# A decoder layer's matrix-state recurrence: its small products issued by array shape

## The chip, the cores and the metric

The kernel runs on one core of a Trainium2 chip. A core has a matrix engine (PE, or TensorE: a 128 x 128 array that multiplies a loaded operand with a streamed one and writes to the accumulation memory, PSUM), a vector engine (DVE), a scalar engine (ACT), a general engine (POOL) and a queue engine (SP); each runs its own instructions in order, and they wait for one another by semaphores. PSUM has eight banks of 128 partitions x 512 fp32. The metric is the device time of one execution, in microseconds.

## What is computed

One layer of a hybrid decoder, for a prompt of 1,024 tokens and for 8 sampled sequences of 8 new tokens each. The input projection feeds three groups of heads; their outputs are projected back, then come a squared-ReLU MLP and a gated embedding. The group that matters here is the first, an RWKV-7 recurrence with a 64 x 64 state per head and four heads:

```python
def wkv7_scan(r, decay, k, v, a_vec, b_vec, s0):
    def step(s, inp):
        r_t, w_t, k_t, v_t, a_t, b_t = inp
        sa = jnp.einsum('bhvk,bhk->bhv', s, a_t)
        s = (s * w_t[:, :, None, :] + sa[..., None] * b_t[:, :, None, :]
             + v_t[..., None] * k_t[:, :, None, :])
        y = jnp.einsum('bhvk,bhk->bhv', s, r_t)
        return s, y
    xs = tuple(jnp.moveaxis(t, 1, 0) for t in (r, decay, k, v, a_vec, b_vec))
    s_final, ys = lax.scan(step, s0, xs)
    return jnp.moveaxis(ys, 0, 1), s_final
```

The prompt starts from a zero state, the sampled sequences from a state that is given. The other two groups are a short gated convolution and stick-breaking attention over the prompt, and over 512 cached tokens for the samples. All of it is fp32; large products are split into a high and a low part in a reduced format and run as three products.

## The kernel before

The kernel is one long program. Its pieces are written down in an order that gives priorities; a planner then fixes the order of each engine's instructions ahead of the run, from its own estimate of every instruction's length: an instruction is placed when its operands and its buffers are free by that estimate, and the earlier one in the text goes first. So independent work fills the gaps: while the recurrence waits for a copy, PE runs matmuls of the projections.

In time, the input norm and the recurrence's inputs come first (to about 195 us), then the prompt's recurrence together with the projections for attention (line 898, and from 376 us the convolution's, lines 171 to 173), then the sampled state (434 to 545 us) together with the convolution and the first attention blocks, then attention, the cached tokens, the MLP (from line 1140) and the last gate.

The recurrence runs over the prompt in 16 chunks of 64 tokens, two at a time (a pair, chunks e = 0 and 1). Heads are kept in pairs: head h = 2j + s, with s the upper or lower 64 partitions.

- `wkv_local` (line 490) prepares a pair without the state. Its first products (line 535) multiply the two kinds of keys (`bk`, 64 rows, 2 x 64 columns) with two streamed rows (`ar`, 64 x 128) for every e, j and s: eight matmuls, those of s = 0 into one bank and those of s = 1 into another, each filling 128 partitions; DVE masks each bank into `AB` (line 538). Transposes (544, 552) and small products (559 to 589) lead to `UV` and `Wm`, and line 600 forms `Rm` and `FT`, one bank for each e. All of this takes turns on PSUM banks 3 and 4, which two such generators share; `TT`, `ar`, `bk`, `AB`, `UV`, `Rm` and `FT` have three buffers.
- `wkv_chain` (line 640) carries the state from chunk to chunk. Line 648 forms the additions to the state (banks 6 and 7). The output of both chunks is collected in one tile of bank 5: for each e and j, line 656 puts in the local part (`UV` with `AB`, all 128 rows of the array, 64 columns, a pair of heads in the two column halves) and line 659 adds the state's part (`St` with `Rm`, 64 rows and 64 columns, a pair of heads on the diagonal quarters). Line 665 multiplies the state by `FT`, and DVE finishes the new state (line 668). Line 673 copies the output, and `wkv_out` normalises it.
- `wkv_sample_chunk` (line 714) does one chunk of 64 sampled tokens. It has PSUM bank 2 alone for everything. It transposes the given states (line 734, loaded into `s_in`), runs `wkv_local` with one chunk, forms the outputs (743, 747), and then, for each j, spreads `UV` and `AB` over the eight sequences with a mask (`um`, line 756; `bmk`, line 762), multiplies them (759: 128 rows; 763: 64 rows, both heads in the upper rows and in the two column halves, with 512 elements streamed each), and finishes the new states (765 to 783). `s_in`, `um`, `FTs` and `so` share two buffers (tag um); `bmk` has one of its own, so that the second `bmk` is made when the first has been read.

A matmul in fp32 leaves two records each for weight load and product in the trace. The transposes of lines 544 and 552 use the whole array.

Of the kernel before, what the change touches and what calls it, by code (L numbers as in the profile page):

```python
# [21 lines left out]
F32 = mybir.dt.float32  # L22
# [10 lines left out]
NB = 8  # L33
# [15 lines left out]
def hybrid_step(ctx: ExitStack, tc: tile.TileContext, I, O):  # L49
    nc = tc.nc  # L50
    V, S, G, PE, SP = nc.vector, nc.scalar, nc.gpsimd, nc.tensor, nc.sync
# [181 lines left out]
    for s in range(2):  # L233
        hs = slice(64 * s, 64 * s + 64)
# [165 lines left out]
    for j in range(2):  # L400
# [9 lines left out]
        for i in range(9):  # L410
            e = min(T, 128 * i + 128)
# [67 lines left out]
    def hp(h):  # L479
        return slice(64 * (h % 2), 64 * (h % 2) + 64)  # L480
# [9 lines left out]
    def wkv_local(cs, res, local, sample=False):  # L490
# [11 lines left out]
        ar = kp.tile([128, ne, 2, 3, 64], F32, name="ar", bufs=1 if sample else 3)  # L502
        bk = kp.tile([128, ne, 2, 2, 64], F32, name="bk", bufs=1 if sample else 3)
# [21 lines left out]
        AB = kp.tile([128, ne, 4, 192], F32, name="AB", bufs=1 if sample else 3)  # L525
        mk = mfull[:, 1 if sample else 0].rearrange("p a t -> p (a t)")[:, None, None, :].to_broadcast([128, ne, 2, 128])

        for both in ((0,), (1,)) if sample else ((0, 1),):
            p4s = {s: local().rearrange("p (e j c) -> p e j c", e=2, j=2) for s in both}
            for e in E:  # L530
                for j in range(2):
                    for s in both:
                        hs = slice(64 * s, 64 * s + 64)
                        ra = ar[hs, e, j, 0:2] if e == 0 else ar[hs, e, j, 2:0:-1]
                        PE.matmul(p4s[s][:, e, j, :], bk[hs, e, j].rearrange("p a t -> p (a t)"), ra,  # L535
                                  start=True, stop=True)
            for s in both:
                V.tensor_mul(AB[:, 0:ne, s:4:2, 64:192], p4s[s][:, 0:ne], mk)
        yield
# [7 lines left out]
        UV = kp.tile([128, ne, 4, 64], F32, name="UV", bufs=1 if sample else 3)  # L547
# [36 lines left out]
        p4 = h4(psv, 512)  # L584
# [13 lines left out]
        for h in range(4):  # L598
            for e in E:
                PE.matmul(j2(prfs[e], 256)[hp(h), h // 2, :], Wm[es(e), h, :], AB[es(e), e, h, 0:128],  # L600
                          start=True, stop=True)
# [37 lines left out]

    def wkv_chain(c, AB, UV, Wm, Rm, FT):  # L640

        py = ybank()
        p4 = py[:, :256].rearrange("p (e j t) -> p e j t", e=2, j=2)
        pg = chain()
        g4 = pg[:, :256].rearrange("p (e j t) -> p e j t", e=2, j=2)
        for e in range(2):
            for h in range(4):
                PE.matmul(g4[hp(h), e, h // 2, :], AB[:, e, h, 0:64], UV[:, e, h, :], start=True, stop=True)
        PG = kp.tile([128, 2, 2, 64], F32, name="PG", bufs=2)
        V.tensor_mul(PG, g4, pcs[:, :, c:c + 2].rearrange("p j e -> p e j")[:, :, :, None].to_broadcast([128, 2, 2, 64]))  # L650
        yield
        for e in range(2):
            St = state[0]
            for j in range(2):
                for h in (2 * j, 2 * j + 1):
                    PE.matmul(p4[hp(h), e, j, :], UV[:, e, h, :], AB[:, e, h, 64:128], start=True, stop=St is None)
                if St is not None:
                    for h in (2 * j, 2 * j + 1):
                        PE.matmul(p4[hp(h), e, j, :], St[hp(h), j, :], Rm[hp(h), e, j, :], start=False, stop=True)
            if St is None:  # L660
                state[0] = PG[:, e]
                continue
            pf = chain()
            for h in range(4):
                PE.matmul(j2(pf)[hp(h), h // 2, :], FT[hp(h), e, h // 2, :], St[hp(h), h // 2, :], start=True, stop=True)
            Sn = kp.tile([128, 2, 64], F32, name="St", bufs=3)
            for j in range(2):
                V.scalar_tensor_tensor(Sn[:, j, :], j2(pf)[:, j, :], pcs[:, j, c + e:c + e + 1], PG[:, e, j, :],
                                       op0=ALU.mult, op1=ALU.add)
            state[0] = Sn  # L670
            yield
        Yg = kp.tile([128, 2, 128], F32, name="Yg", bufs=2)
        S.copy(Yg.rearrange("p j (e t) -> p e j t", e=2), p4)
        yield
        yield from wkv_out(c * 64, 128, Yg, chain)
# [38 lines left out]
    def wkv_sample_chunk(bank):  # L714
        sp = kp
        bm = sp.tile([128, NB, 64], F32, name="bm")
        G.memset(bm, 1.0)
        for s in range(2):
            m = bm[64 * s:64 * s + 64]
            G.affine_select(m, m, pattern=[[-NJ, NB], [0, 64]], compare_op=ALU.is_ge, fill=0.0, base=0,  # L720
                            channel_multiplier=1)
            G.affine_select(m, m, pattern=[[NJ, NB], [0, 64]], compare_op=ALU.is_ge, fill=0.0, base=NJ - 1,
                            channel_multiplier=-1)
        st = I["state_wkv"][0]
        S0 = sp.tile([128, 2, NB, 64], F32, name="S0")
        for j in range(2):
            pt = bank()
            s_in = sp.tile([128, NB, 64], F32, name="s_in", tag="um", bufs=2)
            for s in range(2):
                SP.dma_start(s_in[64 * s:64 * s + 64], st[:, 2 * j + s].rearrange("b v k -> v b k"))  # L730
            for b in range(NB):
                for s in range(2):
                    hs = slice(64 * s, 64 * s + 64)
                    PE.matmul(pt[hs, b * 64:b * 64 + 64], s_in[hs, b, :], ident[hs, hs], start=True, stop=True)
            S.copy(S0[:, j].rearrange("p b v -> p (b v)"), pt)
        res = []
        run(wkv_local((16,), res, bank, True))
        AB, UV, Wm, Rm, _ = res
        Yg = kp.tile([128, 2, 64], F32, name="Yg")
        py = bank()  # L740
        for j in range(2):
            for h in (2 * j, 2 * j + 1):
                PE.matmul(j2(py)[hp(h), j, :], UV[:, 0, h, :], AB[:, 0, h, 64:128], start=True, stop=False)
            for b in range(NB):
                q = slice(b * NJ, b * NJ + NJ)
                for h in (2 * j, 2 * j + 1):
                    PE.matmul(j2(py)[hp(h), j, q], S0[hp(h), j, b, :], Rm[hp(h), 0, j, q], start=False,
                              stop=b == NB - 1)
        S.copy(Yg, j2(py))
        run(wkv_out(NP, 64, Yg, bank))  # L750
        for j in range(2):
            pg, pf = bank(), bank()
            ums = []
            for h in (2 * j, 2 * j + 1):
                um = sp.tile([128, NB, 64], F32, name="um", tag="um", bufs=2)
                V.tensor_mul(um, UV[:, 0, h, None, :].to_broadcast([128, NB, 64]), bm)
                ums.append(um)
            for h, um in zip((2 * j, 2 * j + 1), ums):
                PE.matmul(pg[hp(h), :], AB[:, 0, h, 0:64], um.rearrange("p b v -> p (b v)"), start=True, stop=True)
            for h in (2 * j, 2 * j + 1):  # L760
                bmk = sp.tile([64, NB, 64], F32, name="bmk", bufs=1)
                V.tensor_mul(bmk, AB[0:64, 0, h, None, 0:64].to_broadcast([64, NB, 64]), bm[0:64])
                PE.matmul(pf[hp(h), :], Wm[0:64, h, :], bmk.rearrange("p b k -> p (b k)"), start=True, stop=True)
            FT = sp.tile([128, NB, 64], F32, name="FTs", tag="um", bufs=2)
            V.tensor_add(FT, pf.rearrange("p (b k) -> p b k", b=NB), id128[:, None, :].to_broadcast([128, NB, 64]))
            GS = sp.tile([128, NB, 64], F32, name="GS", bufs=1)
            S.copy(GS.rearrange("p b k -> p (b k)"), pg)
            pn = bank()
            for b in range(NB):
                for s in range(2):  # L770
                    hs = slice(64 * s, 64 * s + 64)
                    PE.matmul(pn[hs, b * 64:b * 64 + 64], FT[hs, b, :], S0[hs, j, b, :], start=True, stop=True)
            V.tensor_add(GS, pn.rearrange("p (b k) -> p b k", b=NB), GS)
            V.tensor_mul(GS, GS, pcs[:, j, 16:24, None].to_broadcast([128, NB, 64]))
            po = bank()
            for b in range(NB):
                for s in range(2):
                    hs = slice(64 * s, 64 * s + 64)
                    PE.matmul(po[hs, b * 64:b * 64 + 64], GS[hs, b, :], ident[hs, hs], start=True, stop=True)
            so = sp.tile([128, NB, 64], F32, name="so", tag="um", bufs=2)  # L780
            S.copy(so.rearrange("p b k -> p (b k)"), po)
            for s in range(2):
                SP.dma_start(wkv_sample[0, :, 2 * j + s].rearrange("b v k -> v b k"), so[64 * s:64 * s + 64])
# [916 lines left out]
```

## Time and profile before

| | |
|---|---|
| median of three runs | 1646.79 us (1643.97 to 1654.39) |
| the profiled execution | 1648.17 us |
| its span, from the first to the last instruction | 1646.5 us |
| first and last prompt record of line 535 | 201.4 and 375.3 us |
| first and last record of line 656 | 234.5 and 414.9 us |
| products of the sampled state, lines 734 to 779 | 433.5 to 536.7 us |

The profile is of one execution. Times in it count from the span's start. A row of a timeline gives when a burst of like instructions began, how long they were busy together, the engine, the line, what is written from what, and the shape. The busy time of one matmul includes the time that its data takes to pass the array, during which the next one has begun; so the busy times of matmuls add up to more than their share of the time, and PE's sequence is better read from one start to the next.

### The profile page before, as it was taken

How to read it: one execution, taken by the hardware profiler on the slowest of the kernel's cores; microseconds unless marked ns; L12 is line 12 of the kernel's file. 1: busy time of each engine (PE TensorE's matmuls, PEld its weight loads, DVE VectorE, ACT ScalarE, POOL GpSimd, SP SyncE). 2: the span in 40 equal slices, each digit the busy share in tenths (PEclk: the TensorE clock that was granted, in tenths of full speed). 3: DMA queues.
4: the chain of work that ended last, by engine and by line, in shares of the span. 5: the costliest groups of instructions: out<-in, count | busy, mean ns of one | idle time of the engine just before them, and what ended most of it. 6: DMA issues, size and time to landing. Idle time of an engine off the chain costs nothing.

```text
span 1646.5 us, 28968 instructions
## 1 busy us (share of the span) xinstructions
PE 1617.9 (98%) x11215; PEld 1402.2 (85%) x11215; DVE 988.6 (60%) x1692; ACT 774.2 (47%) x1502; POOL 713.8 (43%) x793
## 2 busy tenths in 40 slices
PE   6999999999999999999999999999999999999998
PEld 5999777778976777777777789979999999999897
DVE  6367644554467698776344462478776777768332
ACT  7643245333356676665444452474433433437321
POOL 6321202232354664444256614467644554539110
PEclk9999999999999999999999999999999999999999
DMA  5245555434436534332356662223322222223211
GB/s 173 92 134 162 152 134 148 107 101 118 128 111 195 170 99 136 105 109 80 100 185 206 179 208 89 79 65 104 102 90 90 87 81 90 91 78 95 69 47 42
DMA packets 188148, 190.60 MB, mean 116 GB/s; under 512 B 57450, under 2 KB 147338, under 8 KB 187884
## 3 DMA queue, kind: packets, MB, share of 16 engines
q1 hardware_dynamic: 173644, 165.37, 33.6%
q0 software_dynamic: 5472, 16.81, 3.4%
q10 hardware_dynamic: 8896, 6.59, 1.6%
q8 instruction: 88, 1.44, 0.4%
q14 instruction: 48, 0.39, 0.1%
HBM read 154.09 MB, written 34.63 MB: 115 GB/s over the span
## 4 chain that ended last, share of the span: by engine, by line
PE 86%; DVE 6%; DMA 3%; POOL 2%; ACT 2%; issue 1%; SPq 0%; ACTq 0%; POOLq 0%; DVEq 0%
PE b L1140 13%; PE b L1141 13%; PE b L1142 13%; PE b L898 8%; PE b L171 3%; PE b L172 3%; PE b L173 3%; PE b L1498 3%; PE b L1499 3%; PE b L1497 3%; PE b L983 2%; PE b L979 2%; PE b L535 1%; DVE keep L963 1%; DMA wr<-in_w_up 1%
## 5 line engine op out<-in xcount | busy, mean ns | idle before, releaser
L1121 POOL TENSOR_TENSOR wl<-wr,wh 128x512 fp32r<-128x512 f32 x138 | 196.8, 1432 | 230.8 <-ACT wh L1120 227.5
L1541 DVE TENSOR_TENSOR x<-b,x 128x288 f32<-128x288 f32 (+1 forms) x384 | 199.1, 529 | 109.2 <-PE b L1142 107.6
L1120 ACT CAST wh<-wr 128x512 fp32r<-128x512 f32 x234 | 143.4, 621 | 218.0 <-PE b L1141 173.1
L1140 PE MATMUL b<-ah,wh 128*128 128x288 f32 (+1 forms) x612 | 202.6, 332 | 3.1 <-DVE x L1541 2.1
L1141 PE MATMUL b<-al,wh 128*128 128x288 f32 (+1 forms) x612 | 200.7, 328 | 0.2 <-POOL al L1511 0.2
L1142 PE MATMUL b<-ah,wl 128*128 128x288 f32 (+1 forms) x612 | 200.3, 328 | 0.0
L1140 PE MATMUL b<-nh,wh 128*128 128x512 f32 (+1 forms) x352 | 129.8, 369 | 0.3 <-DVE x L1452 0.2
L1141 PE MATMUL b<-nl,wh 128*128 128x512 f32 (+1 forms) x352 | 129.8, 369 | 0.0
L1142 PE MATMUL b<-nh,wl 128*128 128x512 f32 (+1 forms) x352 | 129.3, 367 | 0.0
L1140 PEld LDWEIGHTS b<-ah,wh 128*128 128x128 f32 x612 | 114.9, 188 | 13.8 <-DVE x L1541 3.8
L1141 PEld LDWEIGHTS b<-al,wh 128*128 128x128 f32 x612 | 115.0, 188 | 9.8 <-issue 1.7
L1142 PEld LDWEIGHTS b<-ah,wl 128*128 128x128 f32 x612 | 114.9, 188 | 7.9
L171 PE MATMUL b<-h_hi,wh 128*128 128x384 f32 (+1 forms) x336 | 114.3, 340 | 1.9 <-ACT xs L353 1.1
L963 DVE TENSOR_TENSOR_SCAN keep<-keep,onesq 128x128 f32<-128x128 f32 (+3 forms) x64 | 93.0, 1455 | 35.7 <-POOL keep L961 35.0
L172 PE MATMUL b<-h_lo,wh 128*128 128x384 f32 (+1 forms) x336 | 112.2, 334 | 1.0 <-DVE h_lo L217 1.0
L173 PE MATMUL b<-h_hi,wl 128*128 128x384 f32 (+1 forms) x336 | 111.9, 333 | 0.0
L1121 POOL TENSOR_TENSOR wsl<-s,wsh 128x512 fp32r<-128x512 f32 x60 | 77.3, 1308 | 25.7 <-ACT wsh L1120 25.7
L1121 DVE TENSOR_TENSOR wl<-wr,wh 128x512 fp32r<-128x512 f32 x96 | 76.0, 794 | 18.3 <-ACT wh L1120 17.6
L159 POOL TENSOR_TENSOR wl<-wr,wh 128x512 fp32r<-128x512 f32 x40 | 56.5, 1428 | 59.3 <-ACT wh L156 53.3
L898 PE MATMUL b<-wh,h_hi 128*128 128x512 f32 x192 | 78.0, 407 | 0.0
L898 PE MATMUL b<-wl,h_hi 128*128 128x512 f32 x192 | 76.2, 397 | 0.0
L898 PE MATMUL b<-wh,h_lo 128*128 128x512 f32 x192 | 76.1, 397 | 0.0
(483 smaller groups left out, 4446.1 us busy)
## 6 DMA issues: line engine op xcount, KB each, us to landing
wr<-in_w_up SPq DMA_DIRECT2D x64, 512.0 KB
wr<-in_w_down SPq DMA_DIRECT2D x64, 512.0 KB
wr<-in_w_in SPq DMA_DIRECT2D x26, 512.0 KB
wr<-in_w_out SPq DMA_DIRECT2D x16, 512.0 KB
xt<-in_x_prompt SPq DMA_DIRECT2D x8, 512.0 KB
stk_s<-sth ACTq DMA_DIRECT2D x32, 128.0 KB
stk_s<-stl SPq DMA_DIRECT2D x32, 128.0 KB
stk_q<-stk_s SPq DMA_DIRECT2D x16, 256.0 KB
```

The source lines that it names most:

```text
L159: sub[k0 // step % 2].tensor_sub(lo, raw[:, c:c + 512], f(hi))
L171: PE.matmul(ps[:, :n], wh[k][:, c], a, start=(k == 0), stop=False)
L172: PE.matmul(ps[:, :n], wh[k][:, c], b, start=False, stop=False)
L173: PE.matmul(ps[:, :n], wl[k][:, c], a, start=False, stop=(k == nk - 1))
L898: last = PE.matmul(ps[i], x[:, t0:t0 + 128], wt, start=start, stop=stop)
L963: marks[1] = V.tensor_tensor_scan(keep[:, 0:L][:, ::-1], keep[:, 0:L][:, ::-1], onesq[:, 0:1].to_broadcast([128, L]), 1.0, op0=ALU.mult, o ...
L1120: S.copy(h3, src)
L1121: (sub or G).tensor_sub(l3, src, f(h3))
L1140: PE.matmul(ps[:, :n], w(0, k, m), a, start=(k == 0), stop=False)
L1141: PE.matmul(ps[:, :n], w(0, k, m), b, start=False, stop=False)
L1142: PE.matmul(ps[:, :n], w(1, k, m), a, start=False, stop=(k == nk - 1))
L1541: V.tensor_add(p.x[:, m, t0:t0 + n], ps[:, :n], p.x[:, m, t0:t0 + n])
```

## The change

Three edits, in the three functions named above.

In `wkv_local`, for the prompt, each first product of 64 rows and 128 columns is replaced by two of 64 rows and 64 columns, one for each kind of key (a). Those of one e and j are issued in the order of (s, a): (0, 0), (1, 1), (0, 1), (1, 0). The sampled chunk keeps its products.

In `wkv_chain`, the local parts of the output, of both chunks and all four heads, are issued first, in one run of eight matmuls; the state's part follows for each chunk, four matmuls in a run, and then line 665 as before. The accumulation in bank 5 is opened by the first two matmuls, one for each half of the partitions, and closed by the last two.

In `wkv_sample_chunk`, tag um has three buffers, and `bmk` takes its buffers from it and has none of its own; the two `bmk` of a j are both made before their two products are issued.

```diff
@@ -532,8 +532,13 @@
                     for s in both:
                         hs = slice(64 * s, 64 * s + 64)
                         ra = ar[hs, e, j, 0:2] if e == 0 else ar[hs, e, j, 2:0:-1]
-                        PE.matmul(p4s[s][:, e, j, :], bk[hs, e, j].rearrange("p a t -> p (a t)"), ra,
-                                  start=True, stop=True)
+                        if sample:
+                            PE.matmul(p4s[s][:, e, j, :], bk[hs, e, j].rearrange("p a t -> p (a t)"), ra,
+                                      start=True, stop=True)
+                    for s, a in () if sample else ((0, 0), (1, 1), (0, 1), (1, 0)):
+                        hs = slice(64 * s, 64 * s + 64)
+                        ra = ar[hs, e, j, 0:2] if e == 0 else ar[hs, e, j, 2:0:-1]
+                        PE.matmul(p4s[s][64 * a:64 * a + 64, e, j, :], bk[hs, e, j, a], ra, start=True, stop=True)
             for s in both:
                 V.tensor_mul(AB[:, 0:ne, s:4:2, 64:192], p4s[s][:, 0:ne], mk)
         yield
@@ -650,13 +655,15 @@
         V.tensor_mul(PG, g4, pcs[:, :, c:c + 2].rearrange("p j e -> p e j")[:, :, :, None].to_broadcast([128, 2, 2, 64]))
         yield
         for e in range(2):
+            for h in range(4):
+                PE.matmul(p4[hp(h), e, h // 2, :], UV[:, e, h, :], AB[:, e, h, 64:128], start=e == 0 and h < 2,
+                          stop=False)
+        for e in range(2):
             St = state[0]
-            for j in range(2):
-                for h in (2 * j, 2 * j + 1):
-                    PE.matmul(p4[hp(h), e, j, :], UV[:, e, h, :], AB[:, e, h, 64:128], start=True, stop=St is None)
-                if St is not None:
-                    for h in (2 * j, 2 * j + 1):
-                        PE.matmul(p4[hp(h), e, j, :], St[hp(h), j, :], Rm[hp(h), e, j, :], start=False, stop=True)
+            if St is not None:
+                for h in range(4):
+                    PE.matmul(p4[hp(h), e, h // 2, :], St[hp(h), h // 2, :], Rm[hp(h), e, h // 2, :], start=False,
+                              stop=e == 1 and h >= 2)
             if St is None:
                 state[0] = PG[:, e]
                 continue
@@ -725,7 +732,7 @@
         S0 = sp.tile([128, 2, NB, 64], F32, name="S0")
         for j in range(2):
             pt = bank()
-            s_in = sp.tile([128, NB, 64], F32, name="s_in", tag="um", bufs=2)
+            s_in = sp.tile([128, NB, 64], F32, name="s_in", tag="um", bufs=3)
             for s in range(2):
                 SP.dma_start(s_in[64 * s:64 * s + 64], st[:, 2 * j + s].rearrange("b v k -> v b k"))
             for b in range(NB):
@@ -750,18 +757,20 @@
         run(wkv_out(NP, 64, Yg, bank))
         for j in range(2):
             pg, pf = bank(), bank()
-            ums = []
+            ums, bmks = [], []
             for h in (2 * j, 2 * j + 1):
-                um = sp.tile([128, NB, 64], F32, name="um", tag="um", bufs=2)
+                um = sp.tile([128, NB, 64], F32, name="um", tag="um", bufs=3)
                 V.tensor_mul(um, UV[:, 0, h, None, :].to_broadcast([128, NB, 64]), bm)
                 ums.append(um)
             for h, um in zip((2 * j, 2 * j + 1), ums):
                 PE.matmul(pg[hp(h), :], AB[:, 0, h, 0:64], um.rearrange("p b v -> p (b v)"), start=True, stop=True)
             for h in (2 * j, 2 * j + 1):
-                bmk = sp.tile([64, NB, 64], F32, name="bmk", bufs=1)
+                bmk = sp.tile([128, NB, 64], F32, name="bmk", tag="um", bufs=3)[0:64]
                 V.tensor_mul(bmk, AB[0:64, 0, h, None, 0:64].to_broadcast([64, NB, 64]), bm[0:64])
+                bmks.append(bmk)
+            for h, bmk in zip((2 * j, 2 * j + 1), bmks):
                 PE.matmul(pf[hp(h), :], Wm[0:64, h, :], bmk.rearrange("p b k -> p (b k)"), start=True, stop=True)
-            FT = sp.tile([128, NB, 64], F32, name="FTs", tag="um", bufs=2)
+            FT = sp.tile([128, NB, 64], F32, name="FTs", tag="um", bufs=3)
             V.tensor_add(FT, pf.rearrange("p (b k) -> p b k", b=NB), id128[:, None, :].to_broadcast([128, NB, 64]))
             GS = sp.tile([128, NB, 64], F32, name="GS", bufs=1)
             S.copy(GS.rearrange("p b k -> p (b k)"), pg)
@@ -777,7 +786,7 @@
                 for s in range(2):
                     hs = slice(64 * s, 64 * s + 64)
                     PE.matmul(po[hs, b * 64:b * 64 + 64], GS[hs, b, :], ident[hs, hs], start=True, stop=True)
-            so = sp.tile([128, NB, 64], F32, name="so", tag="um", bufs=2)
+            so = sp.tile([128, NB, 64], F32, name="so", tag="um", bufs=3)
             S.copy(so.rearrange("p b k -> p (b k)"), po)
             for s in range(2):
                 SP.dma_start(wkv_sample[0, :, 2 * j + s].rearrange("b v k -> v b k"), so[64 * s:64 * s + 64])
```

## The prediction

> **What bounds the kernel now.** I read the page first: engines (1), then the chain that ended last (4).
>
> ```profile
> span 1646.5 us, 28968 instructions
> PE 1617.9 (98%) x11215; PEld 1402.2 (85%) x11215; DVE 988.6 (60%) x1692; ACT 774.2 (47%) x1502; POOL 713.8 (43%) x793
> PE 86%; DVE 6%; DMA 3%; POOL 2%; ACT 2%; issue 1%; SPq 0%; ACTq 0%; POOLq 0%; DVEq 0%
> ```
>
> PE is nearly never idle and carries 86% of the chain. The change touches the stage of the recurrence alone, so next comes busy time by stretch (columns: start:end, length, then busy time and instruction count of PE, PEld, DVE, ACT, POOL, then granted clock, DMA share, GB/s).
>
> ```profile
> 195.00:420.00 225.00, 225.00 (x2113) 179.14 (x2112) 104.74 (x230) 90.16 (x188) 53.05 (x58) 1.00 0.48 122
> 440.00:470.00 30.00, 27.87 (x194) 25.21 (x189) 20.62 (x34) 16.38 (x35) 19.57 (x33) 0.94 0.43 127
> 470.00:490.00 20.00, 20.00 (x179) 16.63 (x179) 9.87 (x19) 11.85 (x23) 6.50 (x17) 0.91 0.30 98
> 490.00:545.00 55.00, 54.19 (x404) 38.05 (x401) 38.40 (x60) 35.93 (x78) 28.75 (x60) 1.00 0.65 198
> ```
>
> From 195 to 420 us, where the prompt's recurrence runs between the projections' matmuls of L898, PE never idles, while DVE and ACT are busy less than half. Whatever the small products no longer take of PE's sequence is filled by the next large matmul, so there a microsecond of PE's sequence is a microsecond of the kernel. In the sampled state's part (440 to 545) this holds a little less: PE idles 2.1 us before 470 and the clock is under 1.
>
> Busy time cannot price these products, because matmuls overlap. What counts is the step: from the start of a burst to the start of the next one. So I read the timeline of PE (columns: start, length, engine, line, operation, shape: rows*columns of the array, then partitions x elements streamed; xN is records, and one fp32 matmul leaves two: L535 has 64 matmuls in the eight prompt pairs and 128 records).
>
> ```profile
> 280.70 0.39 PE L898 MATMUL b<-wh,h_hi 128*128 128x512 f32 x1
> 280.93 0.39 PE L898 MATMUL b<-wl,h_hi 128*128 128x512 f32 x1
> 281.24 0.33 PE L659 MATMUL b<-Rm,St 64*64 64x64 f32 x4
> ...
> 282.95 0.48 PE L535 MATMUL b<-ar,bk 64*128 64x128 f32 x2
> 283.37 0.34 PE L656 MATMUL b<-AB,UV 128*64 128x64 f32 x4
> 283.63 0.33 PE L659 MATMUL b<-Rm,St 64*64 64x64 f32 x4
> 283.80 0.40 PE L665 MATMUL b<-St,FT 64*64 64x64 f32 x8
> 284.13 0.34 PE L656 MATMUL b<-AB,UV 128*64 128x64 f32 x4
> 284.39 0.50 PE L898 MATMUL b<-wh,h_lo 128*128 128x512 f32 x1
> ```
>
> A burst of four L656 records takes 0.26 (283.37 to 283.63), L659's four take 0.17 when L665 follows in the same 64*64 shape, L665's eight take 0.33. One step of L898 is 0.23, but 0.31 when a burst of another shape follows (280.93 to 281.24): a change of shape costs about 0.09, which a same-shape sequel doesn't pay.
>
> **The change part by part.**
>
> *Local outputs of both chunks first (wkv_chain).* Before, L656 and L659 alternate by head pair.
>
> ```profile
> 296.35 0.34 PE L656 MATMUL b<-AB,UV 128*64 128x64 f32 x4
> 296.61 0.33 PE L659 MATMUL b<-Rm,St 64*64 64x64 f32 x4
> 296.88 0.33 PE L656 MATMUL b<-AB,UV 128*64 128x64 f32 x2
> 297.13 1.16 PE L535 MATMUL b<-ar,bk 64*128 64x128 f32 x8
> ...
> 384.29 0.33 PE L656 MATMUL b<-AB,UV 128*64 128x64 f32 x2
> ```
> ```profile
> 277.34 0.69 PE L648 MATMUL b<-UV,AB 128*64 128x64 f32 x16
> 277.85 0.29 PE L656 MATMUL b<-AB,UV 128*64 128x64 f32 x4
> 278.07 0.50 PE L898 MATMUL b<-wl,h_hi 128*128 128x512 f32 x1
> ```
>
> The same 128*64 shape twenty records long takes 0.73 (277.34 to 278.07), where five bursts of four would take 5 x 0.26 = 1.30. In sequence, four more records cost (0.73 - 0.26) / 4 = 0.12. L656 has 128 records: ten pieces of two (the first and the last are shown; a piece of two costs as much as four, 0.25) and the equivalent of 27 bursts of four, so 37 x 0.26 = 9.6. After: eight bursts of sixteen at 0.26 + 3 x 0.12 = 0.62, so 5.0. The first pair had its products in long bursts already and gives little, so I take -4.5 of the 4.6.
>
> L659 then stands in one run of eight per chunk, with L665 behind it. Before, per chunk: 0.26 for the first four, which end in a change of shape (296.61 to 296.88 is such a one), and 0.17 + 0.33. After: 0.17 + 0.12 + 0.33 = 0.62 against 0.76, so -0.14 for each of the 15 chunks that have a state: -2.1. Ends for both terms: -4.5 if pieces fall apart again between other work, -8.0 if L656 always follows L648 in its own shape, which saves one more change of shape per pair. The order also asks for the products that need no state before the state is there. Nothing is queued behind a new wait: L656 needs UV, AB and bank 5 only, as before.
>
> *First products in quarters (wkv_local).* Each 64x128 product of the prompt becomes two 64x64 ones, 128 matmuls for 64.
>
> ```profile
> 237.58 0.65 PE L600 MATMUL b<-AB,Wm 64*64 64x128 f32 x8
> 238.17 0.50 PE L898 MATMUL b<-wh,h_lo 128*128 128x512 f32 x1
> 238.60 1.16 PE L535 MATMUL b<-ar,bk 64*128 64x128 f32 x8
> 239.68 0.50 PE L898 MATMUL b<-wh,h_hi 128*128 128x512 f32 x1
> ...
> 403.66 0.66 PE L600 MATMUL b<-AB,Wm 64*64 64x128 f32 x14
> 404.25 0.57 PE L648 MATMUL b<-UV,AB 128*64 128x64 f32 x12
> ```
>
> L535's eight records take 1.08, its two at 282.95 take 0.42: 0.11 for each further record, one after the other. So although the text alternates the two row halves, the schedule does all of one bank (one s) and later all of the other. L600 is the nearest row for the new shape: quarters, with 128 elements streamed. Its eight records take 0.59, and the fourteen at 403.66 also 0.59: the first group, one bank at a time, overlaps two quarters, the second, with both banks open, four. Which does the changed L535 do? The two banks are handed out as before, so a group will again be of one bank: 16 records, two by two. That is 0.59 + 4 further pairs x 0.11 = 1.03 against 1.08, -0.05 for some 14 groups of eight: -0.7, and about -0.3 in the first pair, whose pieces stand apart: -1.0. Ends: -8.0 with four quarters everywhere (seven pairs, 2.16 - 1.03 each) and +14 with none (next part).
>
> The Trainium skill, TensorEngine Tiling (Performance Considerations, Instruction Overhead), speaks against this edit: each matmul has an overhead of about 60 cycles on trn2. As an estimate, 128 more records at 60 cycles of 2.4 GHz (25 ns) would add 3.2 us and turn -1.0 into +2.2, the sum into -6.4. The trace doesn't bear that out for overlapping quarters: fourteen L600 records with 128 elements each fit in 0.59.
>
> *The sampled state.* One more buffer of tag um (bmk's own buffer goes), and both bmk products stand after both bmk are made.
>
> ```profile
> 489.57 1.08 PE L759 MATMUL b<-um,AB 128*64 128x512 f32 x4
> 490.57 0.45 PE L173 MATMUL b<-h_hi,wl 128*128 128x384 f32 x1
> ```
> ```profile
> 492.50 1.07 PE L763 MATMUL b<-bmk,Wm 64*64 64x512 f32 x2
> 493.50 0.44 PE L171 MATMUL b<-h_hi,wh 128*128 128x384 f32 x1
> ...
> 497.74 1.07 PE L763 MATMUL b<-bmk,Wm 64*64 64x512 f32 x2
> ```
> ```profile
> 511.74 1.07 PE L759 MATMUL b<-um,AB 128*64 128x512 f32 x2
> 513.59 1.07 PE L759 MATMUL b<-um,AB 128*64 128x512 f32 x2 [0.42 <-DVE um L756]
> 514.60 0.39 PE L954 MATMUL b<-stk_k,stk_q 128*128 128x256 f32 x1
> ```
>
> A pair side by side costs 1.00 (489.57), one alone costs 1.00 as well (492.50). L759 of j=1 stands apart today; paired it gives -1.0. L763 stands apart four times; each paired half gives -1.0. But the second bmk now waits for L759 to have read the first um, and nothing forces PE to hold the first product until the second is ready. I take one of the two: -2.0 in all, ends 0 and -3.0. On DVE, attention's scan and multiply (L963, L965) are queued behind that second bmk; if it waited the whole of an L759 pair they would be late by 1.0, and PE's L979 waits for them; this is inside the end 0. No DMA moves, and no queue of SP, ACT or POOL gets or loses an instruction.
>
> *Sum:* -4.5 - 2.1 - 1.0 - 2.0 = -9.6. The profiled execution took 1648.17 with 1.7 around its span, 1.4 above the median 1646.79; it would be 1638.6, on the median's scale **1637.2**.
>
> **The rivals.** A measurement of this kernel tells a change of about 1% (16.5 us) from none; smaller ones only by the trace.
>
> *A, slower: quarters do not overlap.* If two quarters of one row half ran one after the other, L535's group would be 1.08 + 8 x 0.11 = 1.96, +0.88 for 16 groups: +14.1. With the other terms, -8.6, this gives 1652.3. It decides from ten serial groups of sixteen. L600's groups of eight speak against it: 0.59, when serial steps of 0.11 would take 1.08. Chance 0.06.
> The Trainium skill would make this so: TensorE: Matmul & The Clock Gate (What overlaps and what doesn't) says that weight loads overlap running matmuls only when the row group differs, and the pairs of one bank share it. L600's 0.59 for eight disagrees, as far as its groups are of one bank.
>
> *B, four quarters at once.* If both banks are free together, as at 403.66, L535 gives -8.0 for -1.0: 1630.2. Against: it happened in one L600 of eight pairs. Chance 0.10.
>
> *C, the time is given back.* The prompt's part gets shorter, but the sampled chain between 440 and 490 waits for its own steps and PE idles more there, at a lower clock.
>
> ```profile
> 460.00:465.00 5.00, 3.97 (x32) 3.69 (x32) 4.40 (x9) 2.20 (x7) 3.56 (x7) 0.78 0.49 154
> 465.00:470.00 5.00, 5.00 (x32) 4.55 (x31) 3.74 (x8) 2.23 (x6) 3.15 (x5) 0.88 0.01 3
> 475.00:480.00 5.00, 5.00 (x39) 4.40 (x38) 0.00 (x0) 3.35 (x8) 0.87 (x4) 0.66 0.24 78
> ```
>
> For it: PE idles there already, and the three rows lose 5 x (0.22 + 0.12 + 0.34) = 3.4 us of clock. Against: the convolution's matmuls (L171) can be drawn forward. If 8 of 9.6 were lost: 1645.2. Chance 0.17.
>
> *D, the planned order shifts.* All engines' order is planned anew from changed lengths, so attention and weight loads after 545 may fall otherwise. Either sign, up to 10 us on a forecast of 1637: 1627 to 1647. PE idles only 28.6 in the whole span, so the gain is the smaller side. Chance 0.12.
>
> **How the numbers follow.** Forecast 0.55, A 0.06, B 0.10, C 0.17, D 0.12. The forecast's own range, from the ends -4.5 to -8.0 for the chain, 0 to -3.0 for the sampled state and 0 to -1.6 for L535, is -4.5 to -12.6: 1634.2 to 1642.3. With B and C and half of D it is 1629 to 1648, which leaves out A and the ends of D. Faster by over 1% (under 1630.3): half of B and some of D and of the forecast, 0.11. Slower by over 1% (over 1663): only a bad plan, 0.02. Within 1%: 0.87.
>
> **What would show each step.** L656 in bursts of sixteen of about 0.62, or behind L648; L659 and L665 together at 0.62 per chunk; the first products with 256 prompt records, in groups of sixteen at 1.03 (A: 1.96; B: thirty-two at 1.03); L759 and L763 x4 at 1.0. The forecast is wrong if those bursts are right and 195 to 420 shortens, but later stretches grow by as much (C, D), or if other work cuts the long bursts into pieces with a change of shape each.

## The result, and the profile after

| | kernel before | changed kernel | ratio (95% interval) |
|---|---|---|---|
| first measurement, six runs each | 1646.80 us | 1636.12 us | 0.9925 (0.9906 to 0.9945) |
| second, 21 and 4 runs | 1649.75 us | 1634.52 us | 0.9908 (0.9894 to 0.9923) |

The change takes 10.7 and 15.2 us off; the two intervals overlap, so the two measurements do not contradict each other. In the page of the changed kernel (first measurement; its profiled execution took 1637.35 us) the span, the engines and the chain's shares read:

```profile
span 1635.7 us, 29216 instructions
PE 1600.7 (98%) x11343; PEld 1395.6 (85%) x11343; DVE 997.5 (61%) x1692; ACT 773.7 (47%) x1502; POOL 709.1 (43%) x793
PE 88%; DVE 6%; DMA 2%; ACT 2%; POOL 1%; issue 1%; SPq 1%; ACTq 0%; POOLq 0%; DVEq 0%
```

PE has 128 records more, 64 matmuls, and is busy 17 us less; it is still the bound. Busy time by stretch of the changed kernel, the same stretches as before:

```profile
195.00:420.00 225.00, 223.41 (x2317) 182.68 (x2317) 115.05 (x240) 93.71 (x195) 59.34 (x68) 1.00 0.49 128
440.00:470.00 30.00, 26.71 (x177) 23.09 (x176) 22.58 (x36) 15.89 (x34) 17.72 (x35) 0.94 0.42 136
470.00:490.00 20.00, 20.00 (x186) 17.03 (x184) 13.68 (x25) 13.46 (x29) 7.41 (x25) 1.00 0.30 96
490.00:545.00 55.00, 51.59 (x396) 37.31 (x395) 36.09 (x52) 34.46 (x75) 27.61 (x53) 1.00 0.67 200
```

Up to 420 us PE idles 1.6 us, where it did not idle before. From 440 to 470 it idles 3.3 us for 2.1, and from 490 to 545 3.4 us for 0.8: a part of what its sequence is spared is lost there. The lower clock of 470 to 490 (0.91) is gone.

The bursts, in PE's timeline of the changed kernel. Lines have moved: first products 535 to 541, `Rm` and `FT` 600 to 605, local outputs 656 to 659, the state's part 659 to 665, the new state 665 to 672, the sampled state's 759 and 763 to 766 and 772.

```profile
238.68 1.09 PE L541 MATMUL b<-ar,bk 64*64 64x128 f32 x16
239.70 0.50 PE L907 MATMUL b<-wh,h_hi 128*128 128x512 f32 x1
...
284.49 0.33 PE L605 MATMUL b<-AB,Wm 64*64 64x128 f32 x2
284.59 0.28 PE L541 MATMUL b<-ar,bk 64*64 64x128 f32 x2
284.65 0.28 PE L605 MATMUL b<-AB,Wm 64*64 64x128 f32 x2
284.69 0.28 PE L541 MATMUL b<-ar,bk 64*64 64x128 f32 x2
284.76 0.28 PE L605 MATMUL b<-AB,Wm 64*64 64x128 f32 x2
284.81 0.28 PE L541 MATMUL b<-ar,bk 64*64 64x128 f32 x2
284.87 0.28 PE L605 MATMUL b<-AB,Wm 64*64 64x128 f32 x2
284.92 0.39 PE L665 MATMUL b<-Rm,St 64*64 64x64 f32 x7
...
290.50 0.69 PE L659 MATMUL b<-AB,UV 128*64 128x64 f32 x16
291.11 0.33 PE L541 MATMUL b<-ar,bk 64*64 64x128 f32 x2
```
```profile
489.15 1.08 PE L772 MATMUL b<-bmk,Wm 64*64 64x512 f32 x4
490.15 0.41 PE L171 MATMUL b<-h_hi,wh 128*128 128x320 f32 x1
...
504.63 1.08 PE L766 MATMUL b<-um,AB 128*64 128x512 f32 x4
505.64 0.49 PE L1149 MATMUL b<-mh,wh 128*128 128x512 f32 x1
...
509.87 1.08 PE L772 MATMUL b<-bmk,Wm 64*64 64x512 f32 x4
510.87 0.50 PE L963 MATMUL b<-stk_k,stk_q 128*128 128x512 f32 x1
```

A group of first products by itself takes 1.02 (238.68 to 239.70). But from 284.49 first products and line 605's products alternate, two records and two, and lead into the state's products of the same shape without the 0.09 of a change: from 284.59 to 284.81 four records of each kind take 0.22, where four of one kind alone would take that. The local outputs stand in sixteens (290.50 to 291.11, 0.61), and the sampled state's products in fours of 1.00.

To add this up, each record of PE is booked with the time to the start of the next one; the table gives the sums by kind of product over 195 to 432 us, in us, worked out from the traces. "Chain" and the like are experiments told below.

| | first products | `Rm`, `FT` | local outputs | state's part | new state | sum |
|---|---|---|---|---|---|---|
| before | 17.1 | 7.8 | 9.5 | 6.5 | 6.0 | 46.9 |
| changed | 12.4 | 6.1 | 5.3 | 5.2 | 5.2 | 34.3 |
| chain alone | 17.5 | 8.4 | 5.2 | 5.1 | 5.4 | 41.6 |
| quarters alone | 13.9 | 6.5 | 9.1 | 6.3 | 4.9 | 40.8 |
| chain and sampled state | 17.3 | 8.4 | 5.2 | 5.1 | 5.4 | 41.4 |
| chain and quarters | 12.6 | 6.2 | 5.3 | 4.9 | 5.2 | 34.3 |
| all, quarters in line | 19.1 | 6.0 | 5.6 | 4.9 | 5.4 | 40.9 |

The second profiles of both kernels, at 1652.34 and 1637.18 us, give the same sums within 0.2, so a difference of 1 us in this table is more than two profiles of one kernel differ by. The changed kernel spares 12.6 here, and 3.1 at the sampled state (lines 759 and 763: 3.0 and 4.0 before, 1.9 and 2.0 after). That is 15.7 of PE's sequence for 10.7 and 15.2 us of time.

### The profile page after: what moved, and what is told of

The parts are those of the page before. It is cut to its first block, busy times and chain, and to the rows that moved or that the text cites. A ratio compares the mean times of both kernels' runs of the same rounds, so it can differ in the third digit from the quotient of the medians.

```text
span 1635.7 us, 29216 instructions
## 1 busy us (share of the span) xinstructions
PE 1600.7 (98%) x11343; PEld 1395.6 (85%) x11343; DVE 997.5 (61%) x1692; ACT 773.7 (47%) x1502; POOL 709.1 (43%) x793
## 4 chain that ended last, share of the span: by engine, by line
PE 88%; DVE 6%; DMA 2%; ACT 2%; POOL 1%; issue 1%; SPq 1%; ACTq 0%; POOLq 0%; DVEq 0%
PE b L1149 14%; PE b L1150 14%; PE b L1151 14%; PE b L907 8%; PE b L1507 4%; PE b L1508 3%; PE b L1506 3%; PE b L171 3%; PE b L172 3%; PE b L173 3%; PE b L992 2%; PE b L988 2%; DMA xt<-in_x_prompt 1%; PE b L1274 1%; DVE keep L972 1%
## 5 line engine op out<-in xcount | busy, mean ns | idle before, releaser
L1130 DVE TENSOR_TENSOR wl<-wr,wh 128x512 fp32r<-128x512 f32 x96 | 75.6, 790 | 17.3 <-ACT wh L1129 16.4
```

Source lines behind the costliest of these rows:

```text
L1130: (sub or G).tensor_sub(l3, src, f(h3))
```

## The experiments

They did not all run on one chip: on two chips the kernel before took 1668.5 to 1669.5 us, on the others 1647 to 1650. Ratios are always to the kernel before on the same chip, at the same time.

**The chain's edit alone**, twice:

```diff
         for e in range(2):
+            for h in range(4):
+                PE.matmul(p4[hp(h), e, h // 2, :], UV[:, e, h, :], AB[:, e, h, 64:128], start=e == 0 and h < 2,
+                          stop=False)
+        for e in range(2):
             St = state[0]
...
```

> The kernel before with the edit of wkv_chain alone: local outputs of both chunks in one run, then the state's part. Theory (each edit gives what its bursts no longer take of PE's sequence, and the planner fills the gap): the local outputs take 5.0 to 5.5 us of PE's sequence for 9.5, the state's part and the next product 10 to 11 for 12.5, so -6 us, ratio 0.996 (0.9945 to 0.998). First rival (the gain needs the quarters, whose shape is the one of the state's products, so that both can run in one stretch): -2 us or less, ratio 0.999. Second rival (what came out is mostly another planned order): any sign, up to 5 us away from -6.

> The chain's edit alone, once more, since its first measurement fell on a chip where the kernel before took 1669.5 us and the later stages waited. Where the kernel before takes about 1650 us: theory (terms of PE's sequence, kept to the end) -5 to -7 us, ratio 0.996; rival 1 (the recurrence's end at 414 us sets the start of the sampled state, and the chain's edit does not move it) -1 to -3 us, ratio 0.9985; rival 2 (no gain, as on the other chip) 1.000.

Measured: 1.0002 (0.9991 to 1.0014), and 1.0023 (1.0013 to 1.0032). PE's sequence is spared 5.3 us, near the theory's 6, but no time; in the second run the medians are 3 us longer (1671.51 for 1668.54). Of the second run's theories rival 2 is the nearest, on these chips.

**The quarters alone**, twice:

```diff
-                        PE.matmul(p4s[s][:, e, j, :], bk[hs, e, j].rearrange("p a t -> p (a t)"), ra,
-                                  start=True, stop=True)
+                        PE.matmul(p4s[s][64 * a:64 * a + 64, e, j, :], bk[hs, e, j, a], ra, start=True, stop=True)
...
```

> The kernel before with the first products in quarters alone. Theory 1, from the changed kernel's trace (quarters share stretches with line 600's products of the same shape and fill their gaps): first products 12.5 to 13.5 us of PE's sequence for 17.1, line 600's 6 to 7 for 7.8, so -5 to -6 us, ratio 0.9965. Theory 2, that of the prediction (two quarters of one bank side by side, nothing else): first products 16 us, time -1 us, ratio 0.9994.

> The quarters alone, once more. Theory (terms of PE's sequence: first products and line 600's together 6 us less) -5 to -7 us, ratio 0.996. Rival 1 (the earlier end of the recurrence, 406 us for 416, counts in full) -9 us or more, ratio 0.9945. Rival 2 (a loss as on the other chip) 1.003.

Measured: 1.0031 (1.0019 to 1.0043), and 1.0025 (1.0015 to 1.0034). Of the sequence 6.1 us are spared, which is theory 1 and not the prediction's 1; but the time gets 4 to 5 us longer by the ratios. Neither theory of the first run had expected that; in the second run rival 2, which had been taken from the first, stands.

**The sampled state's edit alone:**

```diff
-            s_in = sp.tile([128, NB, 64], F32, name="s_in", tag="um", bufs=2)
+            s_in = sp.tile([128, NB, 64], F32, name="s_in", tag="um", bufs=3)
...
-                bmk = sp.tile([64, NB, 64], F32, name="bmk", bufs=1)
+                bmk = sp.tile([128, NB, 64], F32, name="bmk", tag="um", bufs=3)[0:64]
...
```

> The kernel before with the three buffers and the paired products of the sampled state alone. Theory: each of the two lines of products stands as two bursts of four records of about 1.0 us, 3.1 us less of PE's sequence than before; as the stretch from 440 to 490 us waits for its own steps, -1 to -3 us of time, ratio 0.9982 to 0.9994. Rival (the chain of the sampled state is what sets that stretch, and its earlier end lets attention start earlier): -5 us or more, ratio under 0.997.

Measured: 1.0000 (0.9991 to 1.0010), against 0.9982 to 0.9994 by the theory. The planner did not pair the first two products here, as PE's timeline of this kernel shows (line 765 is line 763 before):

```profile
497.57 1.07 PE L765 MATMUL b<-bmk,Wm 64*64 64x512 f32 x2
498.57 0.44 PE L172 MATMUL b<-h_lo,wh 128*128 128x384 f32 x1
...
500.18 1.07 PE L765 MATMUL b<-bmk,Wm 64*64 64x512 f32 x2
```

So the edit in the text does not pair them by itself. The second `bmk` was not what was missing: DVE had finished it at 497.1, before the first of the two products began. The order was fixed ahead of the run from the planner's estimates; which of them put the two apart is not shown. The second two products stand paired here (at 521.1), and in the changed kernel all four do.

**The changed kernel with quarters in line**, twice: the same 64 + 64 products, but those of one bank that follow one another use the same quarter of the array.

```diff
-                    for s, a in () if sample else ((0, 0), (1, 1), (0, 1), (1, 0)):
+            for a in range(0 if sample else 2):
+                for e, j, s in itertools.product(E, range(2), both):
...
```

> The changed kernel with the quarters issued so that those of one bank which follow one another use the same quarter of the array: all of the first kind of key, then all of the second. Theory (the gain of the quarters is that two quarters of one bank run side by side): the groups that stand alone take up to 1.96 us for 1.02, the first products 18 to 26 us of PE's sequence for 12.4, and the time is 5 to 13 us above the changed kernel's, ratio to the kernel before 0.9955 to 1.001. Rival (the shape alone makes the gain, since line 605's and the state's products of the same shape step in between): within 2 us of the changed kernel, ratio 0.9925 to 0.994.

> The changed kernel with quarters that follow one another on the same quarter of the array, once more. Theory (the gain of the quarters needs two of them side by side; in line the first products took 19.1 us of PE's sequence, 12.4 in the changed kernel): 6 to 9 us above the changed kernel, ratio to the kernel before 0.995 to 0.997. Rival (shape alone counts): 0.991 to 0.9925.

Measured: 0.9987 (0.9977 to 0.9998), and 0.9988 (0.9979 to 0.9997). A group by itself, in the timeline of the second:

```profile
237.78 1.58 PE L542 MATMUL b<-ar,bk 64*64 64x128 f32 x16
239.28 0.50 PE L908 MATMUL b<-wl,h_hi 128*128 128x512 f32 x1
```

It takes 1.50 where the changed kernel's takes 1.02, and the first products together 19.1 for 12.4, more than the 17.1 of the kernel before. Side by side is what the quarters gain; the shape alone does not give it. (1.50 and not 1.96: where the group goes from the first kind of key to the second, some records still overlap.) The kernel with chain and quarters, which ran on the same chip as the second of these, took 9.3 us less (1656.56 for 1665.89), although the one in line has the sampled state's edit as well, of which its planned order keeps only a part (the products of lines 759 and 763 before together take 5.0 us in it and 3.9 in the changed kernel). The theory's range of the first run, 0.9955 to 1.001, held; that of the second, 0.995 to 0.997, was too low: more time was lost than the first products' sequence.

**The kernels unchanged, for profiles and a second chip:**

> The kernel before, unchanged, for a profile beside those of the first four runs, in which the kernel before took 1669.5 us, 23 more than in the first measurement. Theory 1 (the extra time is in the later stages: the cached tokens' stage from 815 us waits for instructions that the profile names issue, and the next products wait there too): the recurrence ends at 415 us as in the first profile, and a time of 1669 shows up between 815 and 1080 us. Theory 2 (everything is slower evenly): the recurrence ends at 421. A time of 1647 instead would say that this chip is like the first one; then the stage shows no such waits.

> The changed kernel, unchanged, against the kernel before in the same measurement. If the gain is only what PE's sequence is spared in the recurrence, it is 8 to 12 us wherever the kernel before takes 1647 us, ratio 0.9925 to 0.995. If the kernel before takes 1669 us, and the wait in the later stages has an end of its own, most of the gain is given back there: ratio 0.997 to 1.001.

> The kernel before, for its profile on a chip where it takes 1668 us, if this is such a one. Theory: through 811 us its stages lie within 2 us of those of the profile at 1650, and the 18 us more stand in the cached tokens' stage from 828 us on, as waits named issue at the products of line 1246 and matmuls at a lower granted clock, as the kernel with the sampled state's edit alone showed them. Rival: the waits there come from the edits' order, and the kernel before loses its 18 us evenly. At 1650 it would only repeat the earlier profile.

The kernel before took 1650.66 (ratio 1.0003, 0.9994 to 1.0013) on the chip of the second row of the first table, and 1648.45 (0.9992, 0.9980 to 1.0003) on one more, so neither of these is one of the two at 1669. Its profile from the former, an execution of 1652.34 us, has every line's sum within 2.2 us of the first profile's; among the lines with large products a difference of that size means nothing. The changed kernel's second measurement, 0.9908, lies beyond the 0.9925 to 0.995 that was expected where the kernel before takes 1647 us.

**The changed kernel less the quarters**, so chain and sampled state, on the chip of the second row of the first table:

> The changed kernel without the quarters: first products as before, chain and sampled state as changed. Theory (terms add up): the changed kernel's time plus 5 to 6 us, ratio to the changed kernel 1.0035. Rival (the quarters give nothing that stays): within 2 us of the changed kernel.

Measured: 0.9980 (0.9970 to 0.9990), against 0.9908 for the changed kernel there. The quarters are worth 11.7 us to that kernel (1646.19 less 1634.52), twice what they spare of PE's sequence. The theory of adding terms falls a second time, now upwards.

**The changed kernel less the sampled state's edit**, so chain and quarters:

> The changed kernel without the sampled state's edit: chain and quarters alone. Theory (the sampled state's products give 3.1 us of PE's sequence, of which 1 to 3 stay): ratio to the kernel before 0.992 to 0.9935, the changed kernel's being 0.9908 to 0.9925. Rival (the sampled state's edit gives nothing by itself, and what it seems to give is the order planned around it): 0.991 or less, or over 0.995.

Measured: 0.9926 (0.9913 to 0.9940), on the chip and in the measurement where the chain alone gave 1.0023 and the quarters alone 1.0025. The range holds. The changed kernel itself took 0.9908 and 0.9925 elsewhere, so what the sampled state's edit is worth cannot be told from this.

**What the parts do to each other.** Two ends are worth looking at in this stage: that of the filler (the convolution, line 171; the input projection runs through that line as well, hence the first starts near 20 us) and that of the dependent work (recurrence, sampled state, attention). Here are their records (the count, shortest, median and longest in ns, first and last start), from the views by line, first of the kernel before (the profile with a span of 1650.6 us): the convolution, the new state of the prompt, the last product of the sampled state.

```profile
L171 PE MATMUL b<-h_hi,wh x336: 302/334/687, 20.5 to 509.4; 128*128 128x384 f32 x112, 128*128 128x320 f32 x56
L665 PE MATMUL b<-St,FT x112: 216/218/268, 284.7 to 416.3; 64*64 64x64 f32 x112
L779 PE MATMUL b<-ident,GS x64: 218/218/267, 510.0 to 538.4; 64*64 64x64 f32 x64
```

Then the chain alone (second run):

```profile
L171 PE MATMUL b<-h_hi,wh x336: 302/334/668, 17.7 to 489.5; 128*128 128x384 f32 x112, 128*128 128x320 f32 x56
L667 PE MATMUL b<-St,FT x112: 218/218/267, 281.4 to 414.3; 64*64 64x64 f32 x112
L781 PE MATMUL b<-ident,GS x64: 218/218/268, 514.0 to 539.1; 64*64 64x64 f32 x64
```

the quarters alone (second run):

```profile
L171 PE MATMUL b<-h_hi,wh x336: 302/334/548, 18.0 to 505.3; 128*128 128x384 f32 x112, 128*128 128x320 f32 x56
L670 PE MATMUL b<-St,FT x112: 216/218/267, 278.8 to 405.2; 64*64 64x64 f32 x112
L784 PE MATMUL b<-ident,GS x64: 218/218/267, 507.3 to 539.6; 64*64 64x64 f32 x64
```

and the changed kernel in the second measurement:

```profile
L171 PE MATMUL b<-h_hi,wh x336: 302/334/686, 17.8 to 496.4; 128*128 128x384 f32 x112, 128*128 128x320 f32 x56
L672 PE MATMUL b<-St,FT x112: 216/218/268, 277.6 to 403.2; 64*64 64x64 f32 x112
L788 PE MATMUL b<-ident,GS x64: 218/218/267, 498.4 to 520.7; 64*64 64x64 f32 x64
```

The chain alone ends the filler 20 us earlier (509.4 to 489.5) and the recurrence only 2; the quarters alone end the recurrence 11 us earlier and the sampled state not at all. In both, the sampled state still ends at 539. With all three the recurrence ends 13 us earlier, the filler 13 and the sampled state 18. Chain with quarters ends the recurrence at 403.7, the filler at 495.9 and the sampled state at 534.7, so its gain does not hang on the end of the sampled state. What that means for PE stands in the stretch from 490 to 600 us, one row each of the kernel before, the chain alone, the quarters alone, chain with sampled state, chain with quarters, and the changed kernel:

```profile
490.00:600.00 110.00, 106.86 (x655) 79.51 (x654) 81.04 (x103) 72.38 (x145) 63.64 (x100) 1.00 0.53 161
```
```profile
490.00:600.00 110.00, 99.77 (x586) 69.63 (x585) 81.45 (x92) 71.95 (x140) 60.79 (x94) 0.94 0.52 158
```
```profile
490.00:600.00 110.00, 103.33 (x620) 76.73 (x618) 77.69 (x93) 69.55 (x139) 60.63 (x95) 0.95 0.53 160
```
```profile
490.00:600.00 110.00, 103.12 (x608) 74.34 (x608) 81.96 (x98) 73.76 (x144) 59.95 (x92) 0.95 0.53 162
```
```profile
490.00:600.00 110.00, 106.34 (x654) 76.58 (x656) 80.85 (x95) 75.14 (x151) 65.25 (x94) 1.00 0.53 162
```
```profile
490.00:600.00 110.00, 105.57 (x651) 79.01 (x650) 87.55 (x95) 75.78 (x149) 65.63 (x94) 1.00 0.55 166
```

PE idles 3.1 us of 110 before, 10.2 with the chain alone, 6.7 with the quarters alone, 6.9 with chain and sampled state, 3.7 with chain and quarters and 4.4 with all. In the three kernels that have one of chain and quarters without the other, the clock falls to 0.94 and 0.95. Chain with sampled state ran on a chip where the kernel before takes 1650 us, so this loss does not belong to the chips at 1669. With the chain alone 4.5 of the 10.2 us are waits of attention's first products for ACT (line 956) and 2.6 waits of transposes for a later stage (line 1351); the sampled state's own products wait 1.6. This stretch is where the gain of a part alone goes in the first place. It is read from traces, not shown by an experiment that takes the wait away.

The end of a stage does not show it: attention's last products begin 11 and 9 us earlier with the chain and the quarters alone (802.3 and 804.2 for 813.5). But 192 records of one projection (tiles `ah` and `al`) have run by then, 228 in the kernel before; some 9 us of PE's sequence, worked out from the traces, have only moved behind attention.

**The two chips at 1669 us.** No profile of the kernel before fell on one. The kernel with the sampled state's edit alone, which took the same time there, stands in: its last attention products begin at 812.3 us, 813.5 in the kernel before elsewhere, but its span is 18 us longer (1668.5 for 1650.6). From 815 to 960 us its PE idles 11.2 us at a mean clock of 0.95, where that of the kernel before elsewhere idles nothing at 1.00. PE's timeline in the cached tokens' stage, of the chain alone (second run):

```profile
818.80 0.32 PE L1248 MATMUL b<-kT,Qb 128*32 128x64 f32 x4 [0.81 <-issue]
820.94 0.27 PE L1248 MATMUL b<-kT,Qb 128*32 128x64 f32 x2 [1.83 <-issue]
822.37 0.26 PE L1248 MATMUL b<-kT,Qb 128*32 128x64 f32 x1 [1.16 <-issue]
...
826.11 0.63 PE L1144 MATMUL b<-nh,wl 128*128 128x512 f32 x1
826.53 0.63 PE L1142 MATMUL b<-nh,wh 128*128 128x512 f32 x1
```

PE waits for nothing that the profile names, and the matmuls after it step by 0.42 (826.11 to 826.53), where a 128x512 step was 0.23. Why these chips wait there, and whether a part alone gains on the other chips, stays open: no run of a part alone fell on one of those.

## Why the prediction was right, and where it was not

The forecast was 1637.2, the measured median 1636.12; the ratio of the second measurement, 0.9908, makes 1631.6 of the median before, outside the forecast's own range and inside the stated one. PE as the bound of the recurrence's stretch, and the step from burst to burst as the price, held. That the first measurement came so close is partly luck: more of PE's sequence was spared than forecast (15.7 for 9.6), and less of it became time in that measurement than in the second.

- *Local outputs first.* Predicted -4.5 and -2.1, measured in PE's sequence 9.5 to 5.3 (-4.2), and 12.5 to 10.4 (-2.2) for the state's part with the new state. Bursts of sixteen at 0.61 were predicted at 0.62.
- *Quarters.* This term was mis-sized. The step that failed is "a group will again be of one bank: 16 records, two by two", priced 1.03 for every group and -1.0 in all. Two groups that stand by themselves do take 1.02. But in the new shape most first products join the stretches of line 605 and of the state's products: eight of the sixteen groups take only 0.56 to 0.75. And the two groups of the first pair, which stand by themselves at 203.54 and 204.80, take 0.60 each, four records at once. Together that is 17.1 to 12.4 (-4.6) and line 605's 7.8 to 6.1 (-1.7). I had priced the new shape mostly against its own neighbours in one bank, not against the other products that now have the same shape. The 3.2 us that the estimate put on the 128 more records do not show: the line with these records got 4.6 shorter.
- *Sampled state.* Predicted -2.0 with one of two pairings; both came in the changed kernel, -3.1. By itself the edit paired only two of line 763's four products.
- *Rival A* (quarters of one bank in sequence) did not happen. Brought about by another order of the same products, it costs 0.48 per group by itself and most of the gain of the whole change.
- *Rival B* (four at once everywhere) did not happen in its form, but four records at once did, in the first pair by themselves and later with line 605's as partners.
- *Rival C* (given back later): PE's sequence was spared 15.7, and the first measurement shows 10.7 us of time, the second 15.2. Whether 5 us were given back in the first is not shown, as the intervals overlap. If they were, the right time is a quarters term that was 5 too small and a loss of 5 that was given only a chance of 0.17; if not, the forecast was 5 us short. With a part alone, what is lost is as much as what is spared, or more.
- *Rival D* (the planned order shifts) cannot be told apart from C by the times. The planned order is new in every kernel here, and the quarters being worth 11.7 us for 6.3 of sequence is of the size that D allowed for.
- A second step failed: "there a microsecond of PE's sequence is a microsecond of the kernel". PE's sequence itself does nearly add up (chain -5.3 and quarters -6.1 make -11.4, both together -12.6), but the time does not: either part alone gains none, and both together 12.0 us on the same chip (1656.56 for 1668.54). A spared microsecond counts only as far as PE does not wait for it later, and by the traces it is in the stretch from 490 to 600 us that it does. What makes the planned order wait there with one part and not with both stays open.

The Trainium skill, TensorE: Matmul & The Clock Gate (What overlaps and what doesn't), which would have had weight loads of one row group wait, is not borne out: sixteen records of first products in 1.02, 1.50 when the column half stays the same too, and sixteen of the local outputs, which share all rows, in 0.61. The Trainium skill says on the same page, TensorE: Matmul & The Clock Gate (The HAM clock gate), that after some 3.4 us of idle PE the clock halves until PE has been busy for as long. The steps of 0.42 for 0.23 behind the waits at 818 to 823, where the granted clock is 0.83 (820 to 840), agree with the halving. They do not agree with the 3.4 us: the longest wait there is 1.83.

## What to carry to other kernels

Price a small product by the step to the next burst and not by its busy time, and look for products that could share one array shape: they then overlap with each other as well as with themselves. Issue tiles so that neighbours use different parts of the array; the same products in another order lost most of the gain. In a kernel whose gaps are filled by independent work, a microsecond spared in one stage can come back as a wait in the next, so look at the idle time and the clock behind the change. Here two parts that gained nothing singly gained 12 us together, so try parts together before discarding them.

## What the runs showed of the hardware that had not been expected

The same kernel takes 1647 to 1650 us in three measurements, and 1668.5 and 1669.5 us in two others, on other chips. As far as the traces show, the difference lies behind the attention stage (815 to 960 us: 11.2 us of idle PE and a clock of 0.95, against none and 1.00), in waits that the profile can only name issue, at runs of many small matmuls, and in the lower clock that follows them.
